# Four conditioning units before layer 1's first projection, and the last norm's weights by a broadcast load

## The chip, the cores and the metric

The kernel runs on one core of one Trainium2 chip. A core has a tensor engine (PE, with its weight loads shown as PEld), a vector engine (DVE), a scalar engine (ACT), GpSimd (POOL) and a sync engine (SP) that here only issues loads. Each engine works through its own queue in order. Time is device microseconds of one execution, and lower is better. The trace is that of one profiled execution.

## The reference, cut to what matters

Two layers over 256 tokens of width 1024, in float32. Each layer has a mixer and a mixture of 16 experts, and each of these is preceded by a norm that a conditioning vector shifts, scales and gates:

```python
cond = jax.nn.silu(c)
for l in range(DEPTH):
    mod = (cond @ ada_w[l] + ada_b[l])[:, None, :]
    sh1, sc1, g1, sh2, sc2, g2 = jnp.split(mod, 6, axis=-1)
    h = rmsnorm(x, norm_mix[l]) * (1.0 + sc1) + sh1
    mix = even_mixer(h, ...) if l % 2 == 0 else odd_mixer(h, ...)
    x = x + g1 * mix
    h = rmsnorm(x, norm_ffn[l]) * (1.0 + sc2) + sh2
    x = x + g2 * grouped_moe(h, ...)
return rmsnorm(x, final_norm)
```

`ada_w` is 1024 by 6144 for each layer. `odd_mixer`, that of layer 1, projects `h` to 2064 columns, does gated linear attention over half of the result and pooling over the other half, and projects back. `grouped_moe` routes every token to two experts.

## The kernel before, in words

All engine queues are written out by hand: what the program calls in order is what each engine does in order. Weights come through a ring of 16 buffers of 1 MB (`buffer`, `unit`), loaded on SP's queue; a load waits until an earlier buffer has been used. Large weights are used once, so almost all of the run is a stream of loads with products behind it.

**Conditioning units.** `ada(l, s, n)` computes n of the six parts of `mod[l]`. It is a generator. Each step takes one unit of `ada_w` (1 MB) from the ring and does four products with it into one PSUM bank (L195, eight records in the trace, since a float32 product leaves two). The step with the last unit also has ACT copy the sums to SBUF (L200). One more step transposes them on PE (L204) and adds the bias on POOL. The generators wait in a list, `jobs`; `fill(n)` does n steps of the first job, going on to the next when it ends, and `finish(n)` empties the list down to n jobs. So calls of `fill` between other work set where the units run on PE, and when their loads are asked for on SP.

Layer 1 has three such jobs left when its mixer begins: one of 8 units (10 steps would find it done), and two of 4. In program order the mixer calls `fill` twice before its first projection (one call, `fill(2)`), once before each of the next three projections, `fill(3)` after the fourth projection, then one step at a time between the pieces of the output projection (two in the loop over t, one, four in the loop over h, one in `po.second`). The expert stage of layer 1 does the last steps in `by_token` (a `fill(2)` and a `fill(1)`) while DVE works out the routing.

**The first projection of layer 1.** DVE and ACT finish the norm (`rstd`), make the two halves hT of h block by block (`both`, L351 to L361), and split each weight block into a high and a low half (`split`, L60 on ACT and L61 on DVE). `Projections.__call__` multiplies them (L429, L434). POOL meanwhile builds masks and bands (`odd_consts`). The first block of `w_in` has been asked for on POOL's queue already; the others come on SP's queue, in program order with the conditioning units.

**After the fourth projection** ACT applies silu to two PSUM banks (gsr, L1026). Those banks are then taken by the accumulators of the output projection (`po.open`, products at L464).

**The expert stage** (`moe`) gathers tokens (L1207), multiplies by gate, up and down weights (L1272, L1305), scatters back (L1361), for eight pairs of experts. In layer 1 `rows_of_gate` and `spread` lay out two rows over all 128 partitions: the gate g2 and the weights of the last norm. Both stand in rows of one SBUF tile `arow[1, 5]`. A product with a column that picks the rows (`pick`) copies them to all partitions (L1460), four products in four PSUM banks, and ACT copies the banks into the tile `g2fn` (L1462). The first half of `g2fn` is used by every down product from then on; the second half, the norm's weights, only at the very end (`gained`, L1620).

PSUM tiles that live shortly come from `bank`, which hands out three banks in turn.

Of the kernel before, what the change touches and what calls it, by code (L numbers as in the profile page):

```python
# [7 lines left out]
F32 = mybir.dt.float32  # L8
# [3 lines left out]
AF = mybir.ActivationFunctionType  # L12
# [3 lines left out]
T = 256  # L16
D = 1024
# [12 lines left out]
def trunk(ctx: ExitStack, tc: tile.TileContext, x, c, ada_w, ada_b, norm_mix, norm_ffn,  # L30
# [5 lines left out]
    V, S, G, PE, SP = nc.vector, nc.scalar, nc.gpsimd, nc.tensor, nc.sync  # L36
# [10 lines left out]
    def bank(name, two=False):  # L47
        tag, bufs = ("ps", 2) if two or turn[0] % 3 < 2 else ("pq", 1)
        turn[0] += not two
        return psum.tile([128, 512], F32, tag=tag, name=name, bufs=bufs)  # L50
# [51 lines left out]
    ones = const.tile([128, 128], F32, name="ones")  # L102
    V.memset(ones, 1.0)
    ident = const.tile([128, 128], F32, name="ident")
# [27 lines left out]
    b = bank("vcol")  # L132
# [10 lines left out]
    xT = live.tile([128, 8, T], F32, tag="xT", name="xT")  # L143
    for kk in range(4):
        b = bank(f"xt{kk}").rearrange("p (k t) -> p k t", k=2)
# [33 lines left out]
    arow = {}  # L179
# [43 lines left out]
    def fill(n=1):  # L223
        while n and jobs:
            try:
                next(jobs[0])
                n -= 1
            except StopIteration:
                jobs.pop(0)
# [585 lines left out]
    def odd_mixer(pool, nrm, n11, late, project):  # L815
# [11 lines left out]
        gb = pool.tile([128, T], F32, tag="bs", name="gateb")  # L827
        G.dma_start(gb[0:1], gla_gate_b)
        jobs.extend((ada(1, 2, 2), ada(1, 4, 1), ada(1, 5, 1)))
        fill(2)  # L830
        nrm.gain()
        c = Consts()
        odd_consts(pool, c)
# [11 lines left out]
        for g in range(4):  # L845
            b = bank(f"pl{g}")
# [7 lines left out]
        b = bank("alow")  # L854
        for i in range(2):
            for k in range(8):
                j = k % 4
                PE.matmul(b[32 * j:32 * j + 32, 0:T], lhsT=walow[:, k, :], rhs=hs[i].bitcast(F32)[:, k, :],
                          start=i == 0 and k < 4, stop=i == 1 and k >= 4)
# [197 lines left out]
        for h in range(4):  # L1057
            b = bank(f"ot{h}")
# [93 lines left out]
    def moe(l, pool, nrm, psacc, after, following=None):  # L1152
# [288 lines left out]
        g2row = None  # L1441
        def rows_of_gate():
            for h in range(2):
                n = slice(h * 512, (h + 1) * 512)
                S.dma_start(arow[1, 5][32 * h + 1:32 * h + 2], ada_b[1:2, 5 * D:][:, n])
                S.dma_start(arow[1, 5][32 * h + 2:32 * h + 3], final_norm.rearrange("(o n) -> o n", o=1)[:, n])
            pick = pool.tile([128, 4], F32, name="pick")
            g2fn = live.tile([128, 8 * T], F32, tag="h", name="g2fn", bufs=2).rearrange("p (a n) -> p a n", a=2)
            g2row = g2fn[:, 0]
            return g2row, g2fn, pick  # L1450

        def spread():

            V.tensor_tensor(pick[:, 0:2], ident[:, 0:33:32], ident[:, 1:34:32], op=OP.add)
            V.tensor_tensor(pick[:, 0:2], pick[:, 0:2], ident[:, 64:97:32], op=OP.add)
            V.tensor_copy(pick[:, 2:4], ident[:, 2:35:32])
            for i in range(2):
                for h in range(2):
                    b = acc[2 * i + h]
                    PE.matmul(b, lhsT=pick[:, 2 * i + h:2 * i + h + 1].to_broadcast([128, 128]), rhs=arow[1, 5],  # L1460
                              start=True, stop=True)
                    S.activation(g2fn[:, i, h * 512:(h + 1) * 512], b, AF.Copy)  # L1462

        if l:

# [5 lines left out]
        acc = [psacc.tile([128, 512], F32, tag="pa", name=f"acc{l}{i}") for i in range(4)]  # L1471
# [25 lines left out]
        for pr in range(8):  # L1497
# [8 lines left out]
            if pr == 0:  # L1506
                finish()
                if l:
                    g2row, g2fn, pick = rows_of_gate()
# [36 lines left out]
            if pr == 1 and l:  # L1546
                spread()
# [9 lines left out]
            if pr == 4 and l == 1:  # L1557
                for t in range(2):
                    for k in range(8):
                        PE.matmul(block(acc[2 * t + k // 4], k % 4), lhsT=xT[:, k, t * 128:(t + 1) * 128], rhs=ident,  # L1560
                                  start=False, stop=False)
# [43 lines left out]
    with tc.tile_pool(name="odd", bufs=1) as pool:  # L1605
        odd_mixer(Bufs(pool, t=3, w4=3, g=2), n10, n11, lambda: accumulators(ps1, "ps1"), project)
# [83 lines left out]
```

## Time and profile before

| | us |
|---|---|
| median of three runs | 781.63 |
| lowest and highest run | 779.17, 783.79 |
| the profiled execution | 781.72 |
| its span, first to last instruction | 780.0 |
| PE busy in the span | 720.2 |
| DVE, ACT, POOL busy | 315.1, 235.0, 120.8 |

The profiled execution's time is 1.72 us above its span. The kernel moved 282.45 MB by DMA, 362 GB/s over the span. How to read the rows further down: times are microseconds from the start of the span; a timeline row is start, length, engine, line, operation, out<-in, shapes and count, and in brackets the idle time of the engine just before with what ended it. PEclk is the mean granted clock of PE as a share of full speed.

### The profile page before, as it was taken

The page shows a single profiled execution, that of the slowest core. Times are in us where ns is not written, and L with a number is a line of the kernel's source. Part 1 is how long each engine was busy: PE and PEld are TensorE (multiplying, and loading weights), DVE is VectorE, ACT ScalarE, POOL GpSimd, SP SyncE. Part 2 cuts the span into 40 slices and gives each one's busy share as a digit, 9 for nine tenths or more (in the row PEclk, how much of TensorE's full clock was granted, in tenths as well). Part 3 has the DMA queues.
Part 4 walks back from the last instruction along what each step waited for, and adds up shares of the span by engine and source line. Part 5 has one row for each costly group of instructions (what it writes and reads, how often), then busy time and mean ns, then how long its engine had stood idle before and what let it go on. Part 6 is the DMA issues. An engine that isn't in the chain of part 4 may idle for free. (4 is left out here: it accounts for less than half of the span.)

```text
span 780.0 us, 10577 instructions
## 1 busy us (share of the span) xinstructions
PE 720.2 (92%) x4121; PEld 395.7 (51%) x4121; DVE 315.1 (40%) x567; ACT 235.0 (30%) x441; POOL 120.8 (15%) x168
## 2 busy tenths in 40 slices
PE   6898788898999999999888899999999999999995
PEld 4398643476434434443234577678534335444333
DVE  3459979475204113122114846454512214113214
ACT  3457667454102102111112535453401101001012
POOL 1357658022000000000003600010300000000000
PEclk9999999999999999999999999999899999999999
DMA  8999759953999999999999998497699999999994
GB/s 356 384 373 420 313 196 409 360 204 147 353 411 409 409 410 408 409 409 409 409 408 397 394 411 341 165 394 301 258 379 411 409 408 409 409 410 409 409 407 159
DMA packets 74712, 282.45 MB, mean 362 GB/s; under 512 B 5194, under 2 KB 6438, under 8 KB 69530
## 3 DMA queue, kind: packets, MB, share of 16 engines
q1 hardware_dynamic: 73122, 278.68, 91.1%
q0 software_dynamic: 1344, 2.64, 0.9%
q8 instruction: 34, 0.56, 0.3%
q10 hardware_dynamic: 184, 0.34, 0.1%
q14 instruction: 28, 0.23, 0.1%
HBM read 280.59 MB, written 1.05 MB: 361 GB/s over the span
## 5 line engine op out<-in xcount | busy, mean ns | idle before, releaser
L1272 PE MATMUL g<-w,xg 128*64 128x512 f32 x512 | 114.8, 597 | 1.9 <-DMA w<-in_moe_w_gate_dram 1.8
L1272 PE MATMUL u<-w,xg 128*64 128x512 f32 x496 | 111.3, 595 | 3.9 <-DMA w<-in_moe_w_up_dram 3.0
L1305 PE MATMUL dn<-w,at 128*64 128x512 f32 x448 | 100.2, 596 | 3.0 <-DMA w<-in_moe_w_down_dram 1.8
L1284 DVE TENSOR_TENSOR act<-sg,u 128x512 f32<-128x512 f32 (+1 forms) x18 | 11.1, 628 | 155.8 <-PE u L1272 155.8
L1272 PEld LDWEIGHTS u<-w,xg 128*64 128x64 f32 x496 | 34.7, 137 | 74.4 <-issue 62.7
L1272 PEld LDWEIGHTS g<-w,xg 128*64 128x64 f32 x512 | 35.0, 137 | 68.3 <-issue 60.5
L434 PE MATMUL pj<-hT,g 128*128 128x256 f32 x480 | 61.3, 285 | 6.1 <-DVE g L61 4.8
L61 DVE TENSOR_TENSOR g<-wi,g 128x512 fp32r<-128x512 f32 x72 | 57.0, 801 | 23.6 <-ACT g L60 23.4
L1305 PEld LDWEIGHTS dn<-w,at 128*64 128x64 f32 x448 | 31.4, 137 | 64.0 <-issue 55.4
L434 PEld LDWEIGHTS pj<-hT,g 128*128 128x128 f32 x480 | 57.7, 188 | 10.1 <-DVE g L61 6.9
L464 PE MATMUL po<-cat,g 128*128 128x256 f32 x372 | 52.9, 296 | 3.9 <-ACT gsr L1026 1.7
L60 ACT ACTIVATE g<-wi 128x512 fp32r<-128x512 f32 x72 | 44.4, 626 | 38.2 <-PE pj L434 20.7
L429 PE MATMUL pj<-g,hT 128*128 128x512 f32 x192 | 50.3, 412 | 6.0 <-ACT hT L355 3.1
L464 PEld LDWEIGHTS po<-cat,g 128*128 128x128 f32 x372 | 48.1, 201 | 9.3 <-issue 2.7
L195 PE MATMUL ada<-ad,cond 128*32 128x512 f32 x384 | 49.6, 626 | 3.0 <-DMA ad<-in_ada_w_dram 3.0
L429 PEld LDWEIGHTS pj<-g,hT 128*128 128x128 f32 x192 | 35.6, 193 | 20.1 <-DVE g L61 4.2
L570 DVE SCALAR_TENSOR_TENSOR yc<-yp,epar,yc 128x256 f32<-128x256 f32 x56 | 41.5, 756 | 2.2 <-POOL yc L585 1.7
L585 POOL TENSOR_TENSOR yc<-yc,cv 128x256 f32<-128x256 f32 x45 | 39.2, 872 | 19.7 <-ACT cv L584 12.0
L1295 DVE COPY at<-at 128x512 f32<-128x512 f32 x14 | 9.7, 692 | 67.3 <-PE at L1294 67.3
L1337 ACT ACTIVATE ys<-y 128x512 fp32r<-128x512 f32 x28 | 16.9, 625 | 64.2 <-DVE y L1327 59.3
L1280 ACT ACTIVATE sg<-g 128x512 f32<-128x512 f32 x14 | 8.4, 597 | 89.3 <-PE g L1272 89.3
L1331 ACT ACTIVATE y<-dn,cw 128x512 f32<-128x512 f32 x7 | 4.8, 687 | 100.5 <-PE dn L1305 100.5
(381 smaller groups left out, 869.8 us busy)
## 6 DMA issues: line engine op xcount, KB each, us to landing
w<-in_moe_w_gate_dram SPq DMA_DIRECT2D x64, 1024.0 KB, 15.5
w<-in_moe_w_up_dram SPq DMA_DIRECT2D x62, 1024.0 KB, 18.5
w<-in_moe_w_down_dram SPq DMA_DIRECT2D x61, 1024.0 KB, 18.1
ad<-in_ada_w_dram SPq DMA_DIRECT2D x48, 1024.0 KB, 9.0
wi<-in_w_in_even_dram SPq DMA_DIRECT2D x20, 512.0 KB, 12.2
wi<-in_w_in_odd_dram SPq DMA_DIRECT2D x14, 512.0 KB, 12.5
wo<-in_w_out_even_dram SPq DMA_DIRECT2D x4, 1024.0 KB
wo<-in_w_out_odd_dram SPq DMA_DIRECT2D x4, 1024.0 KB, 18.1
```

What stands on the lines that cost most here:

```text
L60: S.activation(g[0], w, AF.Copy)
L61: (eng or V).tensor_tensor(g[1], w, g[0].bitcast(F32), op=OP.subtract)
L195: PE.matmul(acc[32 * j:32 * j + 32, :], lhsT=cond[:, k, :], rhs=w[:, k - (i if n == 2 else 2 * i), c0:c0 + 512], start=i == 0, stop=i == 4 ...
L429: PE.matmul(bs[t], lhsT=self.h[j][:, k, t * 128:(t + 1) * 128], rhs=g[i], start=k == 0 and p == 0, stop=k == 7 and p == 2)
L434: PE.matmul(bs[c // 2][:, (c % 2) * T:(c % 2 + 1) * T], lhsT=g[i][:, c * 128:(c + 1) * 128], rhs=self.h[j][:, k, :], start=k == 0 and c % ...
L464: PE.matmul(self.acc[kd // 2][:, (kd % 2) * T:(kd % 2 + 1) * T], lhsT=block(g[wi], kd % 4), rhs=cats[ci][:, k, :], start=start and kd % 2 ...
L570: V.scalar_tensor_tensor(yc[:, k], yp[:, k, j:j + T], epar[:, k, j:j + 1], yc[:, k], op0=OP.mult, op1=OP.add)
L585: G.tensor_tensor(y, y, p, op=OP.add)
L1272: PE.matmul(b[64 * e:64 * e + 64, :], lhsT=xg[:, k, o + 64 * e:o + 64 * e + 64], rhs=we[:, e, k % 2 * 512:k % 2 * 512 + 512], start=k == 0 ...
L1284: V.tensor_tensor(a[:, n], sg[:, n], ub[:, n], op=OP.mult)
L1305: PE.matmul(bs[h][64 * e:64 * e + 64, :], lhsT=at[k][:, 64 * e:64 * e + 64], rhs=r[:, e], start=k == 0, stop=k == 3)
L1337: S.activation(ys[:, 0, n], y[h], AF.Copy)
```

## The change

Layer 1's mixer does four steps of the conditioning job before its first projection instead of two, and two products whose result nobody reads follow them on PE. All other calls of `fill` stay as they are. The weights of the last norm are no longer copied by products: one load on POOL's queue writes them to all 128 partitions of the second half of `g2fn`. Two rows of `arow[1, 5]`, two columns of `pick`, two products and two copies of ACT's go.

```diff
@@ odd_mixer
         jobs.extend((ada(1, 2, 2), ada(1, 4, 1), ada(1, 5, 1)))
-        fill(2)
+        fill(4)
+
+        idle = bank("idle1")
+        for _ in range(2):
+            PE.matmul(idle[:, 0:T], lhsT=ones, rhs=xT[:, 0, :], start=True, stop=True)
         nrm.gain()
@@ moe, rows_of_gate
                 S.dma_start(arow[1, 5][32 * h + 1:32 * h + 2], ada_b[1:2, 5 * D:][:, n])
-                S.dma_start(arow[1, 5][32 * h + 2:32 * h + 3], final_norm.rearrange("(o n) -> o n", o=1)[:, n])
-            pick = pool.tile([128, 4], F32, name="pick")
+            pick = pool.tile([128, 2], F32, name="pick")
             g2fn = live.tile([128, 8 * T], F32, tag="h", name="g2fn", bufs=2).rearrange("p (a n) -> p a n", a=2)
             g2row = g2fn[:, 0]
+            G.dma_start(g2fn[:, 1], final_norm.rearrange("(o n) -> o n", o=1).broadcast_to([128, D]))
             return g2row, g2fn, pick
@@ moe, spread
             V.tensor_tensor(pick[:, 0:2], pick[:, 0:2], ident[:, 64:97:32], op=OP.add)
-            V.tensor_copy(pick[:, 2:4], ident[:, 2:35:32])
-            for i in range(2):
-                for h in range(2):
-                    b = acc[2 * i + h]
-                    PE.matmul(b, lhsT=pick[:, 2 * i + h:2 * i + h + 1].to_broadcast([128, 128]), rhs=arow[1, 5],
-                              start=True, stop=True)
-                    S.activation(g2fn[:, i, h * 512:(h + 1) * 512], b, AF.Copy)
+            for h in range(2):
+                PE.matmul(acc[h], lhsT=pick[:, h:h + 1].to_broadcast([128, 128]), rhs=arow[1, 5], start=True, stop=True)
+                S.activation(g2row[:, h * 512:(h + 1) * 512], acc[h], AF.Copy)
```

## Rows read from the trace of the kernel before

**Rows 1.** The page: span, and busy time of the engines.

```profile
span 780.0 us, 10577 instructions
PE 720.2 (92%) x4121; PEld 395.7 (51%) x4121; DVE 315.1 (40%) x567; ACT 235.0 (30%) x441; POOL 120.8 (15%) x168
```

**Rows 2.** Table of stretches: busy time per engine, PEclk, DMA share, GB/s.

```profile
430.00:435.00 5.00, 3.13 (x7) 2.24 (x8) 4.96 (x10) 3.53 (x8) 4.30 (x11) 0.69 1.01 377
505.00:510.00 5.00, 3.30 (x33) 1.50 (x26) 1.76 (x6) 4.86 (x10) 1.67 (x2) 1.00 0.67 228
545.00:550.00 5.00, 4.99 (x39) 3.92 (x42) 1.87 (x11) 1.84 (x6) 0.00 (x0) 0.79 0.02 5
620.00:630.00 10.00, 10.00 (x49) 3.91 (x49) 1.83 (x4) 0.63 (x1) 0.00 (x0) 1.00 1.03 408
```

**Rows 3.** PE's waits, 555 to 780: total us, times, longest.

```profile
PE acc L1207 <- DVE P L1191: 1.0, 1, 1.0
PE dn L1305 <- PEq L1403: 0.6, 1, 0.6
PE dn L1305 <- DVE at_7sq L1295: 0.3, 1, 0.3
```

**Rows 4.** Timeline, PE and ACT around the first projection.

```profile
422.70 3.90 PE L275 MATMUL ss<-sq,ones 128*128 128x256 f32 x16 [0.23 <-ACT sq L270]
426.53 1.93 PE L195 MATMUL ada<-ad,cond 128*32 128x512 f32 x16
431.52 0.51 PE L429 MATMUL pj<-g,hT 128*128 128x512 f32 x1 [3.06 <-ACT hT L355]
...
437.69 0.62 ACT L60 ACTIVATE g<-wi 128x512 fp32r<-128x512 f32 x1
...
440.58 5.61 PE L429 MATMUL pj<-g,hT 128*128 128x512 f32 x23 [0.39 <-DVE hT L361]
```

**Rows 5.** DMA issues between 415.3 and 416: count, KB each, us to landing.

```profile
ad<-in_ada_w_dram SPq DMA_DIRECT2D x2, 1024.0 KB, 9.9
```

**Rows 6.** Waits between 410 and 560, a PSUM bank's.

```profile
PEld py L863 <- DVE alowT L867: 0.9, 1, 0.9
```

**Rows 7.** Timeline behind the fourth projection.

```profile
504.44 2.78 PE L195 MATMUL ada<-ad,cond 128*32 128x512 f32 x24
...
508.76 0.59 ACT L200 ACTIVATE arow<-ada 128x512 f32<-128x512 f32 x1
...
508.92 3.16 PE L464 MATMUL po<-cat,g 128*128 128x256 f32 x24 [1.70 <-ACT gsr L1026]
...
519.41 1.07 PE L195 MATMUL ada<-ad,cond 128*32 128x512 f32 x8
```

**Rows 8.** Timeline at the start of layer 1's expert stage.

```profile
552.19 0.60 ACT L200 ACTIVATE arow<-ada 128x512 f32<-128x512 f32 x1 [1.61 <-PE ada L195]
...
554.71 0.78 PE L1207 MATMUL acc<-P,hn1h 128*128 128x256 f32 x2 [1.01 <-DVE P L1191]
```

**Rows 9.** Timeline, the spread of the two rows.

```profile
597.16 3.70 PE L1460 MATMUL acc<-arow,pick 128*128 128x512 f32 x8
```

**Rows 10.** Waits of SP's queue, 400 to 560.

```profile
SPq L1256 <- PE ada L195: 36.3, 8, 15.3
```

**Rows 11.** Timeline, SP's issues at the start of layer 1's expert stage.

```profile
551.10 1.45 SPq L1256 DMA_DIRECT2D w<-in_moe_w_down_dram  x2
552.60 1.12 SPq L1256 DMA_DIRECT2D more<-in_moe_w_up_dram  x2
560.59 3.38 SPq L1256 DMA_DIRECT2D w<-in_moe_w_down_dram  x2
```

**Rows 12.** Timeline of the last down weights' issues and products.

```profile
744.86 15.57 SPq L1253 DMA_DIRECT2D w<-in_moe_w_down_dram  x6
...
765.53 3.61 PE L1305 MATMUL dn<-w,at_7arow 128*64 128x512 f32 x24
```

**Rows 13.** The page's DMA issues, the 256 KB pieces: us to landing.

```profile
w<-in_moe_w_down_dram SPq DMA_DIRECT2D x4, 256.0 KB, 8.7
```

## The prediction, made before the changed kernel ran

> **What bounds the kernel now.** The page comes first: a span of 780.0 us, with PE busy 92% of it and DVE 40% [rows 1]. The profiled execution took 781.72 us, 1.72 more than its span; the median of the three timed runs is 781.63, so sums made against 781.72 can be read against the median.
>
> A share of 92% is an average over stages, so the table of stretches is read next [rows 2]. From 430 to 435 us PE is busy 3.13 of 5 us at a granted clock of 0.69 while DVE has 4.96: this is the front of layer 1's first projection, and DVE sets it. From 505 to 510 PE has 3.30 and ACT 4.86. From 545 to 550 nothing is loaded (5 GB/s). From 620 to 630, in layer 1's expert stage, PE shows 10.00 of 10 while the DMA engines move 408 GB/s: both are full, so something else must say which of the two waits.
>
> That is the list of PE's waits from 555 us on [rows 3]: three waits, 1.9 us in all, in some 214 us, and none of them for a weight. PE is therefore the queue to follow there: what is taken from its stream or put into it shows at the end, as long as the weights keep up. The weights keep up only just, as the last part shows.
>
> [...]
>
> **The change, part by part.** *In front of the projection.* The two conditioning units there start at 426.53 and take 1.93 us; then PE waits 3.06 us for hT, until 431.52 [rows 4]. Two more units (1.9 us) and two products of 256 columns go into this hole. Eight like products took 3.90 us just before [rows 4], so two cost 1.0. The units need their data. The second unit was issued at 415.6 and took 9.9 us to land, so it was there at 425.5 [rows 5]; at 408 GB/s [rows 2] a unit of 1 MB takes 2.56 us, which puts the third at about 428.1 and the fourth at 430.7. PE is then done at 430.7 + 1.0 + 1.0 = 432.7, 1.2 us after the projection could have begun. This delay hides: later in the same projection PE still waits for DVE (the product at 440.58, released by hT) and only from there runs on without a gap [rows 4]. The eight blocks of w_in queue behind two more units on SP's queue and so land 5.1 us later. The first one needed, by ACT at 437.69 [rows 4], would come at about 433. I take 0 for this part, with bounds of 0 and +0.5 us (if the units land a microsecond later).
>
> What the two products are for can be priced. [...] Since DVE decides, I take nothing. [...]
>
> The unread products also take a turn of the three shared PSUM banks, so every later tile gets the next one. The largest wait that I find on such a tile is 0.9 us, for alowT, at the pooling products [rows 6]: I take 0, bounds -0.5 and +0.5.
>
> *What the same calls do later.* All later calls of fill() stay, so the units come two steps earlier everywhere. In the three projections one unit stands where one stood: no change. After the fourth, fill(3) issued three whole units, 2.78 us from 504.44, in the shadow of a wait: PE could go on only at 508.92, after gsr [rows 7]. After the change the third call's worth of work there is one unit, then the transposes of its result, then a unit of the next job. The transposes need ACT's copy of the sums (L200), which stands behind gsr on ACT's in-order queue and ends at 508.76 + 0.59 = 509.35 [rows 7]. So PE does one unit until 505.4, stands still until 509.35, and everything behind it on PE (the output projection's products, the transposes of the attention output, the second half of the products) waits with it. Where three units had been hidden, one is; the other two are done after 509.35, in the open, at 1.0 us apiece (the one at 519.41 takes 1.07 [rows 7]). Sum: 0.4 (509.35 against 508.92) + 2.0 = +2.4 us on PE up to 547.
>
> The hole also lengthens from 1.7 to 3.9 us. In this trace PE's idle 1.70 us before 508.92 left the clock at 1.00, and its 3.06 us before 431.52 was followed by the lower level. So a fall is to be expected after the longer hole in most runs. [...] I take 0.9 (bounds 0 and 1.55).
>
> The two units that had been left for the start of the expert stage come earlier and leave it. There they had cost PE nothing, because the routing held the gather (PE waits 1.01 us for P), but ACT stood 1.61 us waiting for them before its copy [rows 8]. ACT's copies for hn now come earlier. The gather still follows P, so I take -0.3 (bounds 0 and -1.0). The expert stage then begins 2.4 + 0.9 - 0.3 = 3.0 us late.
>
> *The last norm's weights.* The spread of the two rows over the partitions is eight PE records in 3.70 us [rows 9]. Half goes: -1.8 us, in a stretch in which PE never rests. Two of ACT's four copies, one DVE copy and two 2 KB loads go too; ACT and DVE are mostly idle there (0.63 and 1.83 of 10 us [rows 2]), so this is nothing. The new load is 512 KB of writes, on POOL's queue. Its half of the tile comes free only when the expert weights kept there have been used, so POOL waits; POOL has nothing else to do in this stage (0.00 of 10 [rows 2]) and the values are first read at the end. It takes 512 KB of the stream's time, 1.28 us at 408 GB/s.
>
> On PE alone the sum is 3.0 - 1.8 = +1.2 us.
>
> *The weight stream.* Around 545 us it stands still because its ring is full: SP's issue waited 15.3 us for the last conditioning units and went out at 551.10 [rows 10, 11]. After the change these two loads go out some 15 us sooner, into an empty stream. But then the ring is full again and the next load, at 560.59 before [rows 11], waits for PE's first products. Before, four loads of 1 MB issued around 552 [rows 11] (four times 2.56 us, until past 562) bridged that; after, nothing does, and the stream restarts with PE, 3.0 us late, and carries 1.28 us more. At the end there is little room. The last of the 256 KB pieces, issued near 759.2 (the six issues end at 760.43), lands 8.7 us later, about 768; PE's last block of down products runs from 765.53 to 769.14 [rows 12, 13]. With 0.9 us of room the stream could put the end at 3.0 + 1.3 - 0.9 = +3.4 us; with the old bridge fully worth its 3 us it would add nothing to the +1.2 of PE. I take +1.2 for it, about the middle: the total is +2.4 us.
>
> **The rivals.** *Forecast:* 781.72 + 2.4 = 784.1 us, between -0.9 and +4 of the profiled time.
>
> *First rival, slower:* the clock falls behind the long hole and the stream binds the end in full. 2.4 + 1.55 - 0.3 + 0.5 = 4.15 late at the expert stage, + 1.3 - 0.9 = +4.6: 786.3. For it: the clock's fall after 3.06 us, and the stream's room of under 1 us. Against it: the stream had some microseconds in hand at 560.
>
> *Second rival, faster:* the stream bounds the expert stage, and the two loads moved into its standstill are a gain. Two units of 2.56 us less to carry after 551, against 1.28 more: -3.8, 777.9. It decides as soon as PE waits for weights at all in the expert stage. Against it: no such wait is listed [rows 3]. [...]
>
> *Third rival, next to nothing:* the 2.4 us are swallowed at the routing, because ACT's and DVE's work there, not PE's, sets the gather, and the spread's 1.8 us remain: 780.0. Against it: PE is busy 4.99 of 5 us just before the routing [rows 2], whose inputs PE makes.
>
> **How the numbers follow.** Forecast 0.55, first rival 0.22, second 0.10, third 0.13. The likeliest is 784.1. Its own range is 780.8 to 786; the range that leaves out no more than two in ten reaches to most of the first and third rivals: 779.0 to 787.5. About 0.5%, 3.9 us, is what a measurement of this kernel can tell from no change (the three runs lie 4.6 us apart). Faster by more, under 777.7: half of the second rival and a little of the third, 0.07. Slower by more, over 785.5: most of the first rival and a tail of the forecast, 0.25. Within: 0.68.
>
> **What would show it.** PE without the 3.06 us hole before the first projection, the clock at 1.00 there, and yet the projection's last products at the same time, near 446; a hole of nearly 4 us after the unit that follows the fourth projection; the gather some 3 us later against the same stretch; 4 instead of 8 records in the spread; loads under way where 545 to 550 showed 5 GB/s, and a standstill after them. The prediction is wrong if the first projection ends over a microsecond earlier, if PE finds work in the hole behind the fourth, or if waits for weights appear in the expert stage well before its end.

## The result, and the profile after

The changed kernel takes 788.41 us (median of 8 runs, 786.16 to 792.32) against 781.08 us before on the same chip: a ratio of 1.0093 [1.0074, 1.0113]. It is slower by about 7 us where 2.4 were forecast, and lies just above the range. The profiled execution has a span of 787.4 us against 780.0 [rows 1].

The page of the changed kernel, span and PE:

```profile
span 787.4 us, 10577 instructions
PE 717.3 (91%) x4121; PEld 392.7 (50%) x4121; DVE 315.1 (40%) x566; ACT 234.1 (30%) x439; POOL 120.0 (15%) x169
```

PE's busy time is less than before [rows 1], though the span is longer: the time went into standing still. The table of stretches (busy time of PE, PEld, DVE, ACT, POOL, then granted clock, DMA share, GB/s) shows where. Its first three rows answer to [rows 2] (from 620 to 630 us it is as before: PE 10.00 of 10, 410 GB/s):

```profile
430.00:435.00 5.00, 4.28 (x16) 2.25 (x17) 4.96 (x9) 3.26 (x7) 4.45 (x9) 0.66 1.05 406
505.00:510.00 5.00, 1.78 (x12) 0.76 (x12) 1.62 (x4) 3.87 (x10) 1.89 (x3) 0.89 0.61 210
545.00:550.00 5.00, 4.99 (x44) 4.90 (x43) 0.89 (x3) 0.63 (x1) 0.00 (x0) 0.99 0.41 125
```

and two more, of the routing and the start of layer 1's expert stage:

```profile
550.00:560.00 10.00, 4.46 (x23) 4.06 (x23) 7.87 (x23) 6.76 (x13) 5.39 (x6) 0.50 0.42 165
560.00:570.00 10.00, 8.90 (x43) 5.86 (x45) 3.83 (x12) 1.69 (x3) 0.00 (x0) 0.65 0.11 28
```

The same two stretches before the change:

```profile
550.00:560.00 10.00, 8.12 (x49) 4.92 (x41) 9.03 (x23) 7.24 (x13) 6.42 (x6) 0.76 0.77 271
560.00:570.00 10.00, 10.00 (x54) 4.47 (x52) 2.17 (x4) 1.73 (x3) 0.00 (x0) 1.00 1.02 394
```

PE had 8.12 and 10.00 us in them, at a clock of 0.76 and 1.00, and has 4.46 and 8.90 now, at 0.50 and 0.65. The stream of weights carries 125 GB/s where it stood at 5, and 28 GB/s where it moved 394: the standstill has moved, as forecast.

PE's waits from 555 us on (total us, times, longest), which answer to [rows 3]:

```profile
PE rk L1128 <- DVE mb L1124: 5.5, 1, 5.5
PE u L1276 <- DMA w<-in_moe_w_up_dram: 1.5, 2, 0.9
PE acc L1211 <- DVE P L1195: 1.1, 1, 1.1
```

The first line is new, and no step of the prediction speaks of it: PE stands 5.5 us at the routing until DVE has the mask mb. The second is new too: waits for weights.

The timeline at the places of [rows 4], [rows 7] and [rows 9]:

```profile
427.31 1.06 PE L195 MATMUL ada<-ad,cond 128*32 128x512 f32 x8 [0.42 <-DMA ad<-in_ada_w_dram]
430.72 1.94 PE L195 MATMUL ada<-ad,cond 128*32 128x512 f32 x8 [2.34 <-DMA ad<-in_ada_w_dram]
432.59 1.72 PE L834 MATMUL idle<-xT,ones 128*128 128x256 f32 x4
433.95 11.49 PE L429 MATMUL pj<-g,hT 128*128 128x512 f32 x48
...
503.26 1.06 PE L195 MATMUL ada<-ad,cond 128*32 128x512 f32 x8
508.22 0.75 PE L204 MATMUL acol<-ident,arow 128*128 128x128 f32 x4 [3.90 <-ACT arow L200]
508.90 1.94 PE L195 MATMUL ada<-ad,cond 128*32 128x512 f32 x8
510.77 3.82 PE L464 MATMUL po<-cat,g 128*128 128x256 f32 x24
...
604.48 1.98 PE L1461 MATMUL acc<-arow,pick 128*128 128x512 f32 x4
```

The fourth unit came at 430.7, to the tenth where it was expected, and the projection then ran without a gap. Behind the fourth projection there is the hole of 3.90 us, and behind it the eight products of a unit take 1.94 instead of 1.07 us, at a granted clock of 0.50 from 508.90 to 512.31 us.

**Where the time went, by stage.** Layer 0 and the load ahead of layer 1 vary from one execution to the next (the first unit in front of the projection starts at 423.2 to 427.1 us in the fourteen profiles of the table). So the stages are counted from the last product of the fourth projection on. Each number is the difference of two starts in a timeline, in us: A from that product to the first of the output projection (po); B to the first product of ss; C to rk; D to the first product of g; E to the first down product; F from the first pair's down products to the second's (the spread lies in it); G from the seventh pair's to the last pair's; H from there to the end. Of the names, ss are the sums of squares for the expert stage's norm, lg the router's products, mb DVE's mask of the chosen experts, rk the products that turn mb into each token's place, P the one-hot matrix by which tokens are gathered, and g the gate products.

| kernel | A | B | C | D | E | F | G | H | sum to the end |
|---|---|---|---|---|---|---|---|---|---|
| before | 4.81 | 35.79 | 8.72 | 5.19 | 31.6 | 31.2 | 17.1 | 17.9 | 275.85 |
| changed | 7.84 | 37.14 | 12.03 | 5.09 | 32.5 | 29.4 | 18.9 | 18.1 | 284.51 |
| units_alone | 7.59 | 37.38 | 11.75 | 5.06 | 32.8 | 31.2 | 17.1 | 17.9 | 284.43 |
| norm_alone | 4.81 | 35.79 | 8.71 | 5.23 | 31.6 | 29.4 | 19.9 | 18.1 | 277.00 |
| norm_half | 4.81 | 35.79 | 8.72 | 5.41 | 31.6 | 29.4 | 19.0 | 18.1 | 276.39 |
| norm_late | 4.81 | 35.79 | 8.72 | 5.27 | 31.6 | 29.4 | 18.3 | 19.5 | 276.95 |
| idle_alone | 4.81 | 35.79 | 8.72 | 5.28 | 31.6 | 31.2 | 17.1 | 17.9 | 276.02 |
| before_early | 4.81 | 35.80 | 11.47 | 4.90 | 31.6 | 31.2 | 17.1 | 17.9 | 278.35 |
| hold | 7.27 | 37.67 | 8.59 | 5.68 | 32.5 | 29.5 | 18.7 | 18.1 | 281.45 |
| hot | 6.96 | 36.48 | 11.58 | 5.09 | 32.2 | 29.4 | 17.3 | 18.2 | 280.88 |
| mended | 6.97 | 36.48 | 8.61 | 5.21 | 31.6 | 29.5 | 17.6 | 18.1 | 277.44 |
| one | 4.80 | 35.79 | 8.72 | 5.29 | 31.6 | 29.4 | 20.0 | 18.1 | 277.21 |
| one_old | 4.80 | 38.24 | 10.36 | 5.27 | 31.6 | 31.2 | 17.1 | 17.9 | 280.07 |
| warm | 4.81 | 35.79 | 8.68 | 5.09 | 31.6 | 31.2 | 17.1 | 17.9 | 275.74 |

Between the second pair and the seventh every kernel takes 123.4 to 123.6 us. The changed kernel's 8.7 us over before behind the fourth projection are 4.4 in A and B, 3.3 in C, 0.9 in E, 1.8 in G and 0.2 in H, less 1.8 in F and 0.1 in D.

DVE's rows at the routing show C. Before the change, in the timeline of DVE and POOL:

```profile
552.62 0.19 DVE L1088 TENSOR_TENSOR cmp<-cmp,before 128x32 f32<-128x32 f32 x1
...
552.72 0.17 DVE L1117 TENSOR_SCALAR rank<-rank 128x32 f32<-128x32 f32 x1
...
553.06 0.19 DVE L1120 SCALAR_TENSOR_TENSOR mb<-gs,rank 128x32 bf16<-128x32 f32 x1
...
554.02 4.24 POOL L1164 TENSOR_TENSOR hn1l<-hf,hn1h 128x512 fp32r<-128x512 f32 x3 [1.93 <-ACT hf L1163]
...
554.65 1.18 DVE L1088 TENSOR_TENSOR comb<-sc,mask 128x32 f32<-128x32 f32 x1
```

and after it:

```profile
556.12 3.71 POOL L1168 TENSOR_TENSOR hn1l<-hf,hn1h 128x512 fp32r<-128x512 f32 x3
...
556.26 1.18 DVE L1092 TENSOR_TENSOR cmp<-cmp,before 128x32 f32<-128x32 f32 x1
...
557.37 1.29 DVE L1121 TENSOR_SCALAR rank<-rank 128x32 f32<-128x32 f32 x1
...
558.57 0.17 DVE L1089 TENSOR_REDUCE gs<-cmp 128x8 f32<-128x32 f32 x1
558.78 1.10 DVE L1124 SCALAR_TENSOR_TENSOR mb<-gs,rank 128x32 bf16<-128x32 f32 x1
```

The same three operations, of 0.17 to 0.19 us, take 1.10 to 1.29 us where POOL's subtractions for hn's low parts run beside them. Before, ACT stood 1.61 us for the conditioning units [rows 8], so POOL got its inputs late and its three subtractions fell behind mb; there they lengthened comb, for which PE did not wait. After, those units are gone from this place, ACT is early, POOL is early, and meets DVE on the one chain for which everything waits.

The same collision stood in the trace of before all along, in layer 0, whose routing runs the same code but has no conditioning units between ACT's copies:

```profile
189.55 5.12 POOL L1164 TENSOR_TENSOR hn0l<-hf,hn0h 128x512 fp32r<-128x512 f32 x4 [22.28 <-DVE cmp L1088]
...
191.24 1.00 DVE L1088 TENSOR_TENSOR cmp<-gs 128x32 f32<-128x32 f32 x1
192.28 1.22 DVE L1088 TENSOR_TENSOR cmp<-cmp,before 128x32 f32<-128x32 f32 x1
193.42 1.28 DVE L1117 TENSOR_SCALAR rank<-rank 128x32 f32<-128x32 f32 x1
```

There rk follows ss by 11.58 us, against 8.72 in layer 1: 2.9 us more, about as much as layer 1 paid for the collision after the change. In all fourteen profiles this stretch of layer 0 takes 11.56 to 11.59 us. A smaller part may have been paid in layer 1 too: one operation earlier on the chain (v, L1112) takes 0.82 to 0.87 us beside POOL's first subtraction, in both layers of every profile; what it takes alone, none shows.

Not every operation of DVE is longer beside POOL: between rank with 1.29 and mb with 1.10 us in the changed kernel, the reduction gs takes 0.17 us, where it took 0.19 before. What makes the difference, no run shows.

### The profile page after: what moved, and what is told of

Same layout as the page of the kernel before. It is cut to its first block, busy times and chain, and to the rows that moved or that the text cites. A ratio compares the mean times of both kernels' runs of the same rounds, so it can differ in the third digit from the quotient of the medians.

```text
span 787.4 us, 10577 instructions
## 1 busy us (share of the span) xinstructions
PE 717.3 (91%) x4121; PEld 392.7 (50%) x4121; DVE 315.1 (40%) x566; ACT 234.1 (30%) x439; POOL 120.0 (15%) x169
## 5 line engine op out<-in xcount | busy, mean ns | idle before, releaser
L1276 PE MATMUL g<-w,xg 128*64 128x512 f32 x512 | 116.5, 603 | 1.9 <-DMA w<-in_moe_w_gate_dram 1.7
L1309 PEld LDWEIGHTS dn<-w,at 128*64 128x64 f32 x448 | 31.2, 137 | 64.6 <-issue 55.5
L195 PE MATMUL ada<-ad,cond 128*32 128x512 f32 x384 | 52.0, 647 | 7.0 <-DMA ad<-in_ada_w_dram 7.0
L429 PE MATMUL pj<-g,hT 128*128 128x512 f32 x192 | 48.1, 401 | 2.0 <-DVE g L61 2.0
## 6 DMA issues: line engine op xcount, KB each, us to landing
w<-in_moe_w_up_dram SPq DMA_DIRECT2D x62, 1024.0 KB, 18.2
```

Of the source, the lines that this page charges most:

```text
L195: PE.matmul(acc[32 * j:32 * j + 32, :], lhsT=cond[:, k, :], rhs=w[:, k - (i if n == 2 else 2 * i), c0:c0 + 512], start=i == 0, stop=i == 4 ...
L429: PE.matmul(bs[t], lhsT=self.h[j][:, k, t * 128:(t + 1) * 128], rhs=g[i], start=k == 0 and p == 0, stop=k == 7 and p == 2)
L1276: PE.matmul(b[64 * e:64 * e + 64, :], lhsT=xg[:, k, o + 64 * e:o + 64 * e + 64], rhs=we[:, e, k % 2 * 512:k % 2 * 512 + 512], start=k == 0 ...
L1309: PE.matmul(bs[h][64 * e:64 * e + 64, :], lhsT=at[k][:, 64 * e:64 * e + 64], rhs=r[:, e], start=k == 0, stop=k == 3)
```

## The experiments

Two theories of the unforeseen part. **A:** POOL beside DVE makes the masks late, as just read. **B:** the lower clock does it; in the changed kernel it falls to 0.50 at 549.86 us for 17.07 us and PE's products of lg, on which the routing rests, take 1.87 instead of 1.04 us. All kernels were timed against before on their own chip. The changed kernel's ratio to compare with is 1.0093.

### hold: POOL's subtractions made to wait, in the changed kernel

```diff
-        by_token()
+        tokens = by_token()
+        next(tokens)
...
+        if l:
+            G.tensor_copy(small("held", 1)[:, 0], pos[:, 0, 0:1])
+        next(tokens, None)
         comb = small("comb")
...
                     if l and h + t == 0:
                         fill(2)
+                        yield
             fill(FT[l])
+            yield
```

> The changed kernel, with POOL's last three subtractions for the low parts of hn held back by a small POOL copy that reads pos, so that they begin with P, as they did by chance before the change; nothing is left out. Theory A (POOL's subtractions beside DVE's short operations on the masks make three of these about 1 us longer each: 1.18, 1.29 and 1.10 against 0.19, 0.17 and 0.19 us): the three are back at 0.2 us, rk follows ss by 9.1 instead of 12.0 us, and the time is 2.9 us below that of the changed kernel, near 785.5, or less of a gain where the weight stream takes it back at the end (786 to 787). Theory B (the lower clock before the routing makes it late): the clock is as low as it was, rk stays 12.0 us behind ss, and the time stays at 788.4.

C goes from 12.03 to 8.59, against 8.72 before the change. The clock fell here too, at 551.60 and 558.43 us (0.75 on the mean from 550 to 560, 0.74 from 560 to 570), but the first time only behind lg, so that B's part of the delay is missing as well; *hot* takes the two apart. DVE's rows:

```profile
556.88 0.19 DVE L1092 TENSOR_TENSOR cmp<-cmp,before 128x32 f32<-128x32 f32 x1
556.99 0.17 DVE L1122 TENSOR_SCALAR rank<-rank 128x32 f32<-128x32 f32 x1
...
557.32 0.19 DVE L1125 SCALAR_TENSOR_TENSOR mb<-gs,rank 128x32 bf16<-128x32 f32 x1
```

The three are short again. The profile is 3.1 us shorter behind the fourth projection, but the ratio, 1.0081 [1.0054, 1.0108] from six runs, doesn't stand apart from 1.0093: in time this pair alone proves nothing. *mended* against *hot*, below, does.

### before_early: the converse, in the kernel before

```diff
-                    if l and h + t == 0:
-                        fill(2)
+            if l:
+                fill(2)
             fill(FT[l])
```

> The kernel before, with one thing changed: the two conditioning steps at the routing are emitted behind all eight of ACT's copies for hn, so that ACT no longer stands for them and POOL's last three subtractions begin while DVE is at the masks. No unit is moved, nothing is left out. Theory A (POOL beside DVE makes DVE's short operations on the masks about 1 us longer each): two to four of them go from 0.19 to over 1 us, rk follows ss by 11 to 12 us against 8.7, and the time is 2 to 3 us over before, near 784. Theory B (only a lower clock makes the routing late, and here PE has its units as before): rk stays within 0.5 us of 8.7 behind ss, and the time stays at 781.5.

C goes from 8.72 to 11.47; D is 0.3 shorter and the rest stays. The time is 1.0039 [1.0025, 1.0053], 3.0 us. POOL now runs its four subtractions in one piece, and DVE shows it:

```profile
551.91 0.97 DVE L1088 TENSOR_TENSOR cmp<-gs 128x32 f32<-128x32 f32 x1
552.91 1.19 DVE L1088 TENSOR_TENSOR cmp<-cmp,before 128x32 f32<-128x32 f32 x1
554.02 1.30 DVE L1117 TENSOR_SCALAR rank<-rank 128x32 f32<-128x32 f32 x1
...
555.45 0.19 DVE L1120 SCALAR_TENSOR_TENSOR mb<-gs,rank 128x32 bf16<-128x32 f32 x1
```

```profile
550.22 5.06 POOL L1164 TENSOR_TENSOR hn1l<-hf,hn1h 128x512 fp32r<-128x512 f32 x4 [18.94 <-DVE cmp L1088]
```

POOL ends at 555.28; mb, behind it, is short again. No unit and no load was moved here. But ACT's copy of the units' sums was, behind the copies for hn, and PE's transposes wait for it before rk can run:

```profile
554.10 0.74 PE L204 MATMUL acol<-ident,arow 128*128 128x128 f32 x4 [2.49 <-ACT arow L200]
555.69 0.17 PE L1124 MATMUL rk<-mb,sub 128*128 128x16 bf16 x1 [0.85 <-DVE mb L1120]
```

So this run shows that earlier subtractions make DVE's operations long without the change and without a unit moved, but it doesn't show their price: PE was free only 0.85 us before mb came, so by these rows about 1.9 of the 2.75 us would have come from the later transposes alone. The price is shown by the hold: in C by *hold*, in time by *mended* below. The kernel before was fast at this place because ACT waited, the 1.61 us of [rows 8].

### hot: unread products in the two holes of the changed kernel

```diff
-        fill(3)
+        fill(1)
+        idle = bank("idle2")
+        for _ in range(8):
+            PE.matmul(idle[:, 0:T], lhsT=ones, rhs=xT[:, 0, :], start=True, stop=True)
+        fill(2)
...
             fill(FT[l])
+            if l:
+                idle = bank("idle3")
+                for _ in range(6):
+                    PE.matmul(idle[:, 0:T], lhsT=ones, rhs=xT[:, 0, :], start=True, stop=True)
```

> The changed kernel, with eight more unread products of 256 columns between the unit and the transposes in the hole behind the fourth projection, and six behind the transposes at the routing; nothing is left out. Theory (the lower clock behind the two holes costs what is not the hole itself or DVE's slow operations): the clock is 1.00 behind the first hole, the eight products of units there take 1.0 instead of 1.94 us, and the first pair of the expert stage takes 31.6 instead of 32.5 us: up to 1.9 us below the changed kernel, near 786.5. Rival (the first pair is late because its weights are, the clock is not what counts): the stage from the first product of g to the first down product keeps its 32.5 us, and the time stays within 1 us of 788.4. DVE's slow operations at the routing stay in both.

The time is 1.0059 [1.0041, 1.0078] against the changed kernel's 1.0093. The timeline of PE behind the fourth projection:

```profile
501.95 3.72 PE L1039 MATMUL idle<-xT,ones 128*128 128x256 f32 x16
505.92 0.74 PE L204 MATMUL acol<-ident,arow 128*128 128x128 f32 x4 [0.25 <-ACT arow L200]
506.59 1.06 PE L195 MATMUL ada<-ad,cond 128*32 128x512 f32 x8
507.59 3.16 PE L464 MATMUL po<-cat,g 128*128 128x256 f32 x24
```

The unit takes 1.06, the first 24 products of po 3.16 instead of 3.82. A and B together give back 1.5 us: that was the clock, 0.50 from 508.90 to 512.31 us in the changed kernel and 1.00 from 505 to 515 in *mended*, which has the same products here. What they still have over before, 2.2 and 0.7, is the work in the open. At the routing C loses only 0.45 us, with the clock at its upper level until 555.09 us and cmp, rank and mb as long as in the changed kernel: theory B has 0.45 of the 3.3 us and A the rest. E gives back 0.3 of 0.9, since the clock fell again behind the masks: 0.75 on the mean from 550 to 560 us, 0.90 from 560 to 570. G gives back 1.5 us, which was not expected, and why stays open. It is not that the loads restart earlier against PE: from the first load behind the standstill to the first down product it is 29.6 us in both kernels (567.93 to 597.51, and 563.28 to 592.88).

### mended: both repairs

It is *hot* with the edit of *hold*.

> The changed kernel with both repairs at once: POOL's last three subtractions held back until pos is there, and the unread products in the hole behind the fourth projection (eight) and at the routing (six); nothing is left out. Theory (POOL beside DVE at the masks and the lower clock are two causes that add up, and what is left is the hole of some 2 us and the weight stream): rk follows ss by 8.7 us, the output projection starts some 2.2 us later behind the fourth projection than before the change, and the time is near 782, 1 to 3 us over before. Rival (the one repair uses up the other, or the weight stream at the end takes back what is won): no better than with the products alone, 784 to 785.5 or 4 to 5 us over before.

C is 8.61, E 31.6, A and B as in *hot*: behind the fourth projection 277.44 us, 1.6 over before. The time is 1.0014 [0.9995, 1.0032], against 1.0059 [1.0041, 1.0078] without the hold. The place of the subtractions is the only difference: 4.5 us over before without the hold and 1.6 with it, by the medians, and the intervals stand apart. The causes add up.

### units_alone, norm_alone, idle_alone: the change in its parts

Each is the kernel before with one of the three parts of the change's diff. *units_alone*:

```diff
-        fill(2)
+        fill(4)
         nrm.gain()
```

*norm_alone* is the changed kernel with its front undone:

```diff
-        fill(4)
-
-        idle = bank("idle1")
-        for _ in range(2):
-            PE.matmul(idle[:, 0:T], lhsT=ones, rhs=xT[:, 0, :], start=True, stop=True)
+        fill(2)
         nrm.gain()
```

*idle_alone*:

```diff
         fill(2)
+
+        idle = bank("idle1")
+        for _ in range(2):
+            PE.matmul(idle[:, 0:T], lhsT=ones, rhs=xT[:, 0, :], start=True, stop=True)
         nrm.gain()
```

> Only the four units in front of the projection, without the unread products and with the last norm's weights spread as before. Theory A: the hole behind the fourth projection and the slow routing both stand, 3.2 us at ss and 6.5 us at rk; the spread is back at 3.7 us, so the time is up to 1.8 us over the changed kernel, 788.4 to 790.2, 7 to 9 us over before. Rival (the two unread products or the load move the routing): rk less than 4 us late, and the time under 786.

> Only the load of the last norm's weights to all partitions; the front of the first projection is as it was before. Theory A (all of the loss comes from the units that come earlier; the spread's four products are a gain of 1.8 us on PE): 1.8 us below before, near 779.3, the later stages as before, the spread 4 records in 1.9 us. Rival (the 512 KB more bind the weight stream at the end): waits of PE for weights behind 760 us, the time between before and 1.3 us over it, 781.1 to 782.4.

> Only the two unread products in front of the projection, behind the two units that stood there before. Theory A (DVE sets that stretch): the projection's first product goes from 431.5 to at most 431.5, its last one stays near 445.8, and the time stays within 1 us of before, 780.1 to 782.1. Rival (the products keep the clock up and PE's rate decides there): the projection ends 1.0 to 1.5 us earlier and the time is near 779.7. Another rival (the turn of the three shared banks puts waits elsewhere): over 782.1, with a new wait of PE behind 450 us.

The units alone give 1.0089 [1.0067, 1.0111], 6.4 us over before where 7 to 9 were expected: the whole loss. The load gives 0.9995 [0.9982, 1.0008]: F gains 1.8 us, G loses 2.8, and PE waits for weights four times near the end:

```profile
PE u L1272 <- DMA w<-in_moe_w_up_dram: 2.0, 4, 0.6
```

That is the rival of its expectation in kind. It missed the place (the waits end at 747 to 756 us, not behind 760) and the time, which is no higher than before. The products give 0.9987 [0.9973, 1.0001], no difference that can be told. So the change is the units; the other two parts are worth nothing in time. G is 17.1 with the units alone: two loads moved into the standstill cost the end nothing and gave it nothing either.

### norm_half and norm_late: why the load eats the spread's gain

Both are *norm_alone* with one more edit. *norm_half* leaves out half of the load:

```diff
-            G.dma_start(g2fn[:, 1], final_norm.rearrange("(o n) -> o n", o=1).broadcast_to([128, D]))
+            G.dma_start(g2fn[:, 1, 0:512], final_norm.rearrange("(o n) -> o n", o=1)[:, 0:512].broadcast_to([128, 512]))
...
-                V.tensor_tensor(y[:, t, h], acc[2 * t + h], fn[:, n], op=OP.mult)
+                V.tensor_tensor(y[:, t, h], acc[2 * t + h], fn[:, 0:512], op=OP.mult)
```

> Only the load of the last norm's weights, and only the first 512 of its 1,024 columns: 256 KB are loaded, the other half is left out and the second half of the output is multiplied by the first half's weights. Theory (what counts is the time that the load takes in the weight stream): half the bytes give back some 0.6 us of the wait before the last pair's down products, 19.2 to 19.4 us from the sixth pair's down products to the seventh's against 19.9 with the whole load and 17.1 before; the time 0.5 to 1 us below that with the whole load. Rival (the bytes are not it: the earlier PE simply meets the end of a stream that is as long as before): 18.9 us or more as with the whole load less at most 0.2 us, that is 19.7 to 19.9.

*norm_late* has the load in another place:

```diff
-            G.dma_start(g2fn[:, 1], final_norm.rearrange("(o n) -> o n", o=1).broadcast_to([128, D]))
...
         at = actT(7, 0, a, *(live.tile([128, 512], F32, tag=tag, name=f"at{l}_7{tag}", bufs=bufs)
                              for tag, bufs in (("sq", 2), ("arow", 1))))
+        if l:
+            G.tensor_copy(g2fn[:, 1, 0:1], at[0][:, 0:1])
+            G.dma_start(g2fn[:, 1], final_norm.rearrange("(o n) -> o n", o=1).broadcast_to([128, D]))
```

> Only the load of the last norm's weights (front of the projection as before), and this load held back behind a small POOL copy that reads the last pair's activations, some 4 us before the last down products; nothing is left out. Theory A (the load costs because its 512 KB stand in the stream in front of the last weights): the waits of PE for weights behind 745 us are gone or under 1 us, and the halved spread shows: 1.3 to 1.9 us below before, near 780. Rival (the wait moves: the first product with the norm's weights waits for the load, or the last weights still share the queues with it): a wait of DVE or PE of 1 us and more at the end, and the time within 1 us of before, 780.5 to 782.5.

With half the bytes G (in the expectation the pairs are counted from 0) is 19.02, 0.84 less than with all (0.6 were expected), at a time of 0.9989 [0.9971, 1.0008]; in time the two can't be told apart. So the bytes in the stream are a part of the price. They may not be all of it: if the other half gave back as much, 1.1 of the 2.8 us would be left, an estimate from these two G. That PE, 1.8 us sooner by the shorter spread, meets the end of a stream of unchanged length was not tried alone. Held back, the load still has a price. G is 18.3, and H 19.5 where all others have 17.9 to 18.2; there PE waits behind the last down weights:

```profile
763.49 0.35 PEld L1305 LDWEIGHTS dn<-w,at_7arow 128*64 128x64 f32 x4 [0.51 <-DMA w<-in_moe_w_down_dram]
...
765.81 0.65 PE L1305 MATMUL dn<-w,at_7arow 128*64 128x256 f32 x4 [0.66 <-SPq L1403]
```

The time is 1.0010 [0.9998, 1.0023]. The wait moved, as the rival said.

### one and one_old: nothing pushed out of the hole

*one* is the changed kernel with this edit behind the fourth projection, so that later units stand where they stood before. *one_old* has the front of the change and this edit, and the last norm's weights as before.

```diff
         rs = rs[0]
-        fill(3)
+        fill(1)
         pj.close()
```

> The changed kernel with one call less at the fourth projection: one step of the units there instead of three, so that from there on each unit stands where it stood before the change, the two at the routing too; nothing is left out. Theory A (the loss is the two units that no longer fit behind the fourth projection and the work that is missing at the routing): the output projection's first product comes at most 1.5 us later behind the fourth projection than before the change, rk follows ss by 8.7 us, and the time is 781.5 to 783.5, some 5 to 7 us below the changed kernel. Rival (four units at the front, or their loads, cost something by themselves): 785 or more.

> The kernel before with four units and the two unread products in front of the projection, and one step instead of three behind the fourth projection; the last norm's weights are spread as before. Nothing is left out. Theory A (the front is free, and so is the hole behind the fourth projection when no work is pushed out of it; what the same kernel with the load loses, it loses to the load at the end): pj to po 4.8 us, rk 8.7 us behind ss, the last pair's down products not held by weights, and the time within 1 us of before. Rival (units early in the stage cost something that the one profile did not show): 2 us or more over before, 782.5 and up.

In *one* the first po comes 4.80 us behind the fourth projection, as before, and C is 8.72: with nothing to do between the last unit and gsr, PE loses nothing there. Only G is longer, by the load. But the times are 1.0038 [1.0024, 1.0051] and 1.0030 [1.0010, 1.0050], 2 to 3 us over before, which is the rival of *one_old*'s expectation. The two profiles tell of one reason. Both have the same hole of 3.41 us. First *one*, then *one_old*, in the timeline of PE:

```profile
507.31 3.16 PE L464 MATMUL po<-cat,g 128*128 128x256 f32 x24 [3.41 <-ACT gsr L1030]
```

```profile
506.11 5.49 PE L464 MATMUL po<-cat,g 128*128 128x256 f32 x24 [3.41 <-ACT gsr L1030]
```

In the second the clock fell inside the hole, at 505.02, for 6.83 us (0.66 on the mean from 505 to 515, where *one* has 1.00), and B is 2.45 us longer; it fell again at 545.98, for 6.83 us (0.66 from 545 to 555), and C is 1.64 us longer. *one*'s profiled execution took 781.42 us, the second shortest of its twelve times; the three shortest go with a mean granted clock of 0.984 to 0.986, the other nine (782.01 to 785.38) with 0.972 to 0.980. That fits a clock that falls behind this hole in most executions, but it was only seen in one profile. What the front itself costs in the timed runs was not measured apart from it. In the profiles it costs little: from the first unit to the last product of the fourth projection it is 77.59 us before, 77.61 with the units alone, 77.96 and 77.97 in the changed kernel and in *one_old*, and 77.16 to 77.22 in the six others that have the two unread products (*one* among them).

### warm: products where the kernel before stands still

The kernel before, with the edit of *idle_alone* and this one behind rk, in both layers:

```diff
+        idle = bank(f"idle2{l}")
+        for _ in range(2):
+            PE.matmul(idle[:, 0:T], lhsT=ones, rhs=xT[:, 0, :], start=True, stop=True)
         mask = small("mask")
         V.tensor_copy(mask, mb)
```

> The kernel before with unread products of 256 columns at two kinds of places where TensorE stands still for about a microsecond: two in front of layer 1's first projection, and two behind rk at each layer's routing, where it waits for P. Nothing is left out. Theory (the clock falls behind those waits, and the gather behind rk runs at the lower level for 3.4 us in the profile): no fall at the gather, g's first product 0.5 to 1.5 us sooner behind rk in each layer, and the time 1 to 2.5 us below before. Rival (POOL's subtractions or the weights, not TensorE's rate, set the gather): g's first product stays 5.2 us behind rk, or comes later by the products' own length, and the time stays within 1 us of before.

The time is 0.9979 [0.9961, 0.9997], 779.05 against 781.66 us: the only kernel here whose interval lies below before, by little; that of *idle_alone*, whose edit it contains, overlaps with it. The profile shows where it gains: at layer 0's gather. First before, then *warm*, in the timeline of PE:

```profile
195.08 0.18 PE L1124 MATMUL rk<-mb,sub 128*128 128x16 bf16 x1 [2.48 <-DVE mb L1120]
...
200.00 1.94 PE L1272 MATMUL g<-w,xg 128*64 128x512 f32 x8
```

```profile
193.72 0.18 PE L1128 MATMUL rk<-mb,sub 128*128 128x16 bf16 x1 [2.43 <-DVE mb L1124]
...
197.17 1.94 PE L1279 MATMUL g<-w,xg 128*64 128x512 f32 x8
```

Before, the clock fell to 0.50 at 196.4 us for 3.41 us, in the gather; here it stays up by the times of the products, two of which take 0.40 instead of 0.63 us, and g follows rk by 3.45 instead of 4.92 us, the upper end of what was expected. The gain lasts: from layer 0's rk to its first down product this profile takes 38.2 us and the other thirteen 39.7 to 39.8, and to the norm's first sums in layer 1 (L275) 226.4 against 227.6 to 228.6. That this is the whole of what the timed runs gain is not shown. In layer 1 the theory failed: the gather runs at the upper level as well (0.40 us for two products, 0.63 before), but then PE waits 0.85 us for ACT's copy out of PSUM, D is 5.09 against 5.19, and the stages behind the fourth projection are as before (275.74).

## Why the prediction was wrong

Forecast was +2.4 us; the median shows +7.3 and the profile, from the fourth projection on, +8.7 (it stood 1.2 ahead there: 1.6 from layer 0, which the change doesn't touch, less 0.4). Step by step:

- **In front of the projection, 0: right.** The fourth unit landed at 430.7, PE was 1.2 us late for the projection by 432.7 in the forecast and 2.4 us in the profile (433.95 against 431.52), because the clock was 0.50 from 430.39 to 433.80 us and the fourth unit and the two products took 3.2 us (430.72 to 433.95) instead of 2.0. It hid behind DVE but for 0.4 us, within the bounds: from the first unit to the last product of the fourth projection 77.96 against 77.59 us. That the clock would stand at 1.00 there was wrong, and cost little.
- **The hole behind the fourth projection, +2.4: right in its mechanism, 0.45 short.** With the clock kept up, A and B are 2.85 us longer (*mended*).
- **The clock behind that hole, +0.9, bounds 0 to 1.55: under-sized.** Changed against *hot* it is 1.5, near the upper bound. No run shows the 1.55 us, nor the 0.9 taken from it; they were the author's estimate. What the runs show in their place is a clock of 0.50 for 3.41 us behind the hole, and those 1.5 us.
- **The routing, -0.3 with bounds 0 and -1.0: the step that failed, in its sign.** The step saw that ACT's copies would come earlier and counted this as a gain or nothing. It took the time of P as given ("the gather still follows P") and did not ask what the earlier copies release: POOL's subtractions, which then run beside DVE's masks and make P itself late. Measured +3.3, of which *hot* leaves 2.9 to POOL beside DVE and gives 0.45 to the clock. The sign and the size could have been read from the trace of before: comb takes 1.18 us beside POOL, against 0.17 to 0.19 for the short operations around it, and layer 0's routing, where ACT does not wait, has the same three long operations and 2.9 us more than layer 1's.
- **Not priced at all:** the lower clock in the first pair of the expert stage (0.65 on the mean from 560 to 570 us, 1.00 before), +0.9.
- **The spread, -1.8: right**, 1.8 in F.
- **The weight stream, +1.2: 1.8 in G.** Its reason was partly wrong. The emptied bridge around 552 does not bind (*units_alone* has 17.1 in G as before); what costs comes with the load: G is 2.8 us longer with the units in their old places (a part of it by the load's bytes, *norm_half*), 1.8 in the changed kernel and 0.2 with the clock kept up (*hot*).

The sum by these sizes: 2.85 + 1.5 + 3.3 - 0.1 (D) + 0.9 - 1.8 + 1.8 + 0.2 (H) = 8.65, of 8.66.

The first rival had the right direction, by the clock and the stream, but not the routing. The second, the stream as the bound from 555 us on, fell: moving two loads out of it gave nothing (G is 17.1 with the units alone, as before). The third assumed that the routing would swallow the delay; the routing added to it.

## What to carry to other kernels

When work leaves a place, follow what its engine now releases sooner, to the last engine in the chain, and ask whether that meets a critical chain on a neighbour: a wait that looks like waste, as ACT's 1.61 us here, can be what keeps two engines apart. Small operations that sit on a critical chain are to be looked for, in the trace at hand, beside the other engine's long ones, even where they cost nothing so far, as comb with its 1.18 us here; where the same code runs twice, as in two layers, the other place may show the price already. The repair that follows from this, the hold in layer 0 of the kernel before, was not run. The broadcast load of 512 KB took 1.8 us off PE here (F in *norm_alone*), but cost 2.8 us in G, 0.84 of them by half of its bytes (*norm_half*), at the end of a stream of weights for which the forecast had estimated 0.9 us of room. In time no difference can be told: 0.9995 [0.9982, 1.0008].

## What was not expected of the hardware

- DVE operations of 0.17 to 0.19 us took 0.97 to 1.30 us beside POOL's subtractions of some 1.3 us; reductions among them stayed at 0.17 to 0.19.
- The granted clock stayed at its lower level, 0.50, for 17.07 us in the changed kernel, from 549.86 on. In the 5 us before it PE had been busy 4.99 of 5 us, in short products, among them 16 of one column each. Before the change a like fall lasted 3.41 us, with two conditioning units behind it.
- The same hole of 3.41 us, with the same work on both sides, saw no fall in one profile (1.00 from 505 to 515 us in *one*); in another (*one_old*) the clock fell inside it, for 6.83 us (0.66 there).
